# Queries, keys and values computed channel-major by the seven-product scheme, in two token halves

## The chip, the cores and the metric

One core of one Trainium2 chip. The kernel is one program with five engines that are ordered by semaphores: PE (matmul), DVE (vector), ACT (scalar, activation functions), POOL (GpSimd) and SP, which here only issues DMAs. The metric is the device time in microseconds of a run of the whole kernel, and lower is better. Time before: median 2371.23 us of three runs (2369.54 to 2375.56).

## The reference

One decoder block on 2048 tokens of 1024 channels, everything in float32. The input is normalised and modulated, projected once to 10240 columns, and split:

```
h = rms_norm(x, norm_w) * (1 + scale) + shift          # shift, scale, gate = silu(c) @ w_ada + b_ada
a, b, g_conv, q, k, v, g_attn, m_conv, m_attn = split(h @ w_in)
u = silu(layer_norm(depthwise_conv31(a * sigmoid(b)))) * silu(g_conv)
y_conv = u @ w_conv_out
q, k = rope(rms_norm(q, q_norm_w)), rope(rms_norm(k, k_norm_w))     # 12 heads of 128 channels
o = softmax-weighted sum over 3 groups of dilated_window_attention(q, k, v)
y_attn = (o * silu(g_attn)) @ w_attn_out
out = x + gate * ((sigmoid(m_conv) * y_conv + sigmoid(m_attn) * y_attn) @ w_out)
```

The three attention groups of four heads have dilations 1, 4 and 16: tokens are grouped by residue, and in each residue class a block of 128 queries attends to its own and the previous block of 128 keys. With dilation 16 a class has 128 tokens, one block. Groups 1 and 2 (dilations 4 and 16) leave an unnormalised result with its minimum and sum; group 0 comes last and joins the three.

## The kernel before

Every float32 product is made of three matmuls: weights and activations are split into a high part (rounded to fp32r by ACT) and a low part (the rest, a subtraction on DVE or POOL), and high x high, high x low and low x high are added up in PSUM.

**Start (0 to about 50 us).** x is loaded by tokens, squared and scaled on ACT, turned by PE (`pt_x` L288, `pt_first` L297); `shift` and `scale` come from products with 32 columns (L314). h stays in SBUF, channel-major, as quarters (two halves of the channels, four pieces of 512 tokens).

**Queries, keys, values (to about 1077 us).** Per head u (12, in the order of groups 1, 2, 0) and block j of 128 tokens, `project_step` makes q, k and v of the block token-major: `z_tokens` L549 does 24 matmuls of 128x384 (8 channel pieces x 3), h as the stationary side. ACT takes the sums of squares from PSUM (L572), POOL the inverse root (`rsqrt_cols` L114, L115), DVE scales from PSUM (L586) and rotates (L593 to L596). Heads of groups 1 and 2 store the block in DRAM (`qkv_d`) and load it again by residue class. Inside each set of 24 matmuls stand hooks, in which one block of attention is done in five stages, each for another block (`attend_step`): `turn_qk` L620 (two transposes), `scores` L635 with the minimum on DVE L645 and exp on ACT L647, `turn_p` L652 with its copy on DVE L654, `values` L684, `turn_o` L675. For group 0 DVE also joins the groups (L661 to L668, L686). In other hooks DVE makes the sums of h's quarters (S1 to S4, L853), which go to DRAM.

**Gates (to about 1930 us).** The columns of a, b and the gates are made channel-major in quads: 256 columns x 1024 tokens by seven products instead of eight (`quad` L1081). A quad has seven slots; in each PE does 12 matmuls of 128x512 (L1091), with weights as the stationary side. Column pieces are loaded and, in the first token half, combined into differences T1 to T4 (POOL, L1046), split (ACT L1054, DVE or POOL L1055) and the differences stored for the second half. `prepare` does this seven slots ahead, with eight buffers for split weights. A quad has its sum in three PSUM banks: `pa` (tag "z"), `pb` (tag "s") and `pc` (tag "o"), two buffers of each tag; ACT copies from `pa` to scratch (L1097), DVE adds `pb` (L1104) and `pc` (L1118), POOL adds L1115. The depthwise convolution runs on DVE, 1.5 to 3.1 steps per slot, with its sums in PSUM (tag "t"; L1140, L1153, L1169). The last blocks of attention take every second of the first 13 slots.

**Tail (to 2368 us).** Layer norm, the two output projections (L1399), merge, and output quads (L1681).

PE's instructions run in the written order (`manual_schedule`). Those of the other engines are placed by a scheduler; each engine takes its queue in order, and a waiting instruction holds up what is behind it.

## Time and profile before

| | before |
|---|---|
| median of 3 runs | 2371.23 us (2369.54 to 2375.56) |
| the profiled execution | span 2368.3 us, from its first to its last instruction; the median of the runs is 2.9 us above it |
| busy PE / DVE / ACT / POOL | 2325.8 / 1737.0 / 1020.9 / 836.1 us |
| granted TensorE clock | 1.00 in nearly every stretch |
| DMA | 378.57 MB, 160 GB/s on average |

Busy is the time in which an engine has an instruction in work. PE overlaps neighbouring matmuls, so the duration of one (349 ns for 128x384) is longer than the distance to the next one's start; what a matmul costs is that distance. Lines of groups give: line, engine, operation, output<-inputs, shape, count, then busy us and mean ns, and after the bar the idle time of the engine just before them with who ended it. Lines of a timeline give start and duration in us.

### The profile page before, as it was taken

The page shows a single profiled execution, that of the slowest core. Times are in us where ns is not written, and L with a number is a line of the kernel's source. Part 1 is how long each engine was busy: PE and PEld are TensorE (multiplying, and loading weights), DVE is VectorE, ACT ScalarE, POOL GpSimd, SP SyncE. Part 2 cuts the span into 40 slices and gives each one's busy share as a digit, 9 for nine tenths or more (in the row PEclk, how much of TensorE's full clock was granted, in tenths as well). Part 3 has the DMA queues.
Part 4 walks back from the last instruction along what each step waited for, and adds up shares of the span by engine and source line. Part 5 has one row for each costly group of instructions (what it writes and reads, how often), then busy time and mean ns, then how long its engine had stood idle before and what let it go on. Part 6 is the DMA issues. An engine that isn't in the chain of part 4 may idle for free.

```text
span 2368.3 us, 38785 instructions
## 1 busy us (share of the span) xinstructions
PE 2325.8 (98%) x12421; PEld 2083.0 (88%) x12421; DVE 1737.0 (73%) x4104; ACT 1020.9 (43%) x2825; POOL 836.1 (35%) x976
## 2 busy tenths in 40 slices
PE   6999999999999999999999999999999999999999
PEld 4899999999999999997888888788888888878887
DVE  7855655555556777776699999989968768787654
ACT  5733343343344555456444444544444444332221
POOL 4321111111111111123677778656556730000221
PEclk9999999999999999999999999999999999999999
DMA  7733544454552222144535445745444569876552
GB/s 279 241 116 117 160 125 144 149 169 149 158 162 67 60 80 67 47 123 154 170 135 176 160 152 195 241 130 151 139 150 134 165 213 330 292 236 204 185 167 102
DMA packets 354121, 378.57 MB, mean 160 GB/s; under 512 B 27688, under 2 KB 249176, under 8 KB 353918
## 3 DMA queue, kind: packets, MB, share of 16 engines
q1 hardware_dynamic: 312622, 314.05, 42.6%
q10 hardware_dynamic: 41296, 62.05, 7.5%
q8 instruction: 99, 1.62, 0.3%
q14 instruction: 104, 0.85, 0.1%
HBM read 235.34 MB, written 140.64 MB: 159 GB/s over the span
## 4 chain that ended last, share of the span: by engine, by line
PE 88%; DMA 4%; DVE 4%; ACT 2%; issue 1%; POOL 1%; SPq 0%; ACTq 0%; DVEq 0%; POOLq 0%
PE pz L549 31%; PE paab L1091 7%; PE yc L1399 6%; PE oa L1681 4%; PE pcab L1091 4%; PE pag_mc_d L1091 4%; PE pag_g_d L1091 3%; PE pag_ma_d L1091 3%; PE po L684 3%; PE ps L635 3%; PE ya L1399 2%; PE pcg_g_d L1091 2%; PE oc L1681 2%; PE pbab L1091 2%; PE paag L1091 2%; PE pcg_mc_d L1091 2%
## 5 line engine op out<-in xcount | busy, mean ns | idle before, releaser
L549 PE MATMUL pz<-wh_u,hT_lo 128*128 128x384 f32 x1504 | 525.2, 349 | 2.5 <-DVE hT_lo L371 2.4
L549 PE MATMUL pz<-wh_u,hT_hi 128*128 128x384 f32 x1504 | 505.6, 336 | 1.3 <-ACT hT_hi L369 1.3
L549 PE MATMUL pz<-wl_u,hT_hi 128*128 128x384 f32 x1504 | 505.8, 336 | 0.0
L114 POOL TENSOR_SCALAR st<-st 128x2 f32<-128x2 f32 x192 | 44.9, 234 | 797.0 <-ACT sq L572 796.7
L586 DVE SCALAR_TENSOR_TENSOR qk<-pz,st,wqk 128x128 f32<-128x128 f32 x384 | 116.9, 346 | 265.0 <-POOL st L115 260.8
L549 PEld LDWEIGHTS pz<-wh_u,hT_lo 128*128 128x128 f32 x1504 | 283.2, 188 | 4.0 <-DVE hT_lo L371 3.7
L549 PEld LDWEIGHTS pz<-wh_u,hT_hi 128*128 128x128 f32 x1504 | 283.8, 189 | 2.2 <-ACT hT_hi L369 1.9
L549 PEld LDWEIGHTS pz<-wl_u,hT_hi 128*128 128x128 f32 x1504 | 282.8, 188 | 0.5 <-issue 0.5
L627 ACT ACTIVATE qkT<-ptq 128x256 f32<-128x256 f32 x192 | 73.8, 384 | 358.1 <-PE ptq L620 302.5
L1169 DVE SCALAR_TENSOR_TENSOR ce<-us,pair_taps,ce 128x512 f32<-128x512 f32 x240 | 180.9, 754 | 6.5
L1140 DVE SCALAR_TENSOR_TENSOR ce<-ut,chan,ce 128x512 f32<-128x512 f32 x240 | 179.8, 749 | 0.0
L1055 POOL TENSOR_TENSOR slT<-wT,shT 128x512 fp32r<-128x512 f32 x107 | 143.8, 1345 | 79.8 <-ACT shT L1054 79.5
L1153 DVE SCALAR_TENSOR_TENSOR cq<-ut,chan,cq 128x512 f32<-128x512 f32 x208 | 156.0, 750 | 1.0
L1054 ACT ACTIVATE shB<-wB 128x512 fp32r<-128x512 f32 x130 | 82.1, 631 | 161.7 <-PE paab L1091 51.7
L115 POOL TENSOR_TENSOR st<-st,mhalf 128x2 f32<-128x2 f32 x192 | 140.1, 729 | 15.9
L572 ACT ACTIVATE sq<-pz 128x128 bf16<-128x128 f32 x384 | 106.1, 276 | 78.7 <-PE pz L549 68.9
L1054 ACT ACTIVATE shT<-wT 128x512 fp32r<-128x512 f32 x110 | 69.4, 631 | 160.9 <-POOL wT L1046 32.0
L1055 POOL TENSOR_TENSOR slB<-wB,shB 128x512 fp32r<-128x512 f32 x85 | 111.9, 1317 | 76.1 <-ACT shB L1054 73.8
L684 PE MATMUL po<-lv,pT 128*128 128x128 f32 x596 | 96.8, 274 | 0.0
L684 PEld LDWEIGHTS po<-lv,pT 128*128 128x128 f32 x596 | 90.9, 190 | 0.6 <-issue 0.5
L593 DVE TENSOR_TENSOR t<-qk,tab 128x256 f32<-128x256 f32 x192 | 82.5, 430 | 5.7
L1055 POOL TENSOR_TENSOR slT<-wB,shT 128x512 fp32r<-128x512 f32 x57 | 75.1, 1324 | 28.4 <-ACT shT L1054 28.3
(783 smaller groups left out, 6163.2 us busy)
## 6 DMA issues: line engine op xcount, KB each, us to landing
wB<-in_w_in_dram SPq DMA_DIRECT2D x154, 256.0 KB, 3.2
qkv_d<-qkv SPq DMA_DIRECT2D x128, 192.0 KB, 2.3
wT<-tT_d SPq DMA_DIRECT2D x88, 256.0 KB, 2.7
tT_d<-wB ACTq DMA_DIRECT2D x66, 256.0 KB, 2.7
lqk<-qkv_d SPq DMA_DIRECT2D x128, 128.0 KB, 2.3
raw_u<-in_w_in_dram SPq DMA_DIRECT2D x84, 192.0 KB, 3.6
acc_d<-osb SPq DMA_DIRECT2D x128, 65.0 KB, 2.0
part<-acc_d ACTq DMA_DIRECT2D x64, 130.0 KB, 2.4
```

Of the source, the lines that this page charges most:

```text
L115: nc.gpsimd.tensor_tensor(dst, scratch[:, :n], mhalf[:, :n], op=ALU.pow)
L549: nc.tensor.matmul(pz[:, :width], part(a, k, P * j, P), w[:, :width], start=(m == 0), stop=(m == 23))
L586: nc.vector.scalar_tensor_tensor(qk[:, 2 * i : 2 * i + 2].rearrange("p a b -> p (a b)"), pz[:, P * i : P * i + P], st[:, 2 + i : 3 + i], w ...
L684: nc.tensor.matmul(po[:, :P], box["pT"][:, P * i : P * i + P], vt, start=(i == 0), stop=(i == nk - 1))
L1054: nc.scalar.activation(h, q[name], AF.Copy)
L1055: eng.tensor_tensor(l, q[name], h.bitcast(F32), op=ALU.subtract)
L1091: nc.tensor.matmul(ps, w, x, start=(m == 0 and ps.name not in first), stop=(m == 11 and not more), skip_group_check=True)
L1140: stt(box["e"], e[:, 1 + j : 513 + j], chan[:, cb, 2 * j : 2 * j + 1], box["e"], op0=ALU.mult, op1=ALU.add)
L1153: stt(box["o"], o[:, 2 + j : 514 + j], w, psum_o, op0=ALU.mult, op1=ALU.add)
L1169: stt(dst, box["both"][:, 1 + j : 513 + j], pair_taps[:, cb, j : j + 1], box["e"], op0=ALU.mult, op1=ALU.subtract if j == 0 else ALU.add)
L1399: nc.tensor.matmul(pz, w, xx, start=(m == 0), stop=(m == len(terms) - 1))
L1681: nc.tensor.matmul(ps, y, w, start=(m == 0 and ps.name not in begun), stop=(m == 11 and not more), skip_group_check=True)
```

## The change

**Projection.** `z_tokens`, `project_step` and the token-major q, k and v are gone. The columns of q, k and v are made by the same `quad` as the gates (now L260, matmul L270). A head pair has three quads for a half of 1024 tokens: 256 columns of q, of k and of v. The host permutes the columns of q and k, so that one 128-column piece holds the first 64 channels of both heads and the other the last 64. Each token half does 18 such quads and then its 22 gate quads, 40 jobs of seven slots; before, the halves were split only for the gates. The host also lays w_in out in 128-column tiles and gives x a second time, channel-major.

**After a quad.** `turn_v` (L447) turns v by 16 transposes in the four slots after the quad. `rotate` (L467) takes q and k: squares on ACT, sums over a head's 128 channels by f32 matmuls with the 32-column matrix `sel` (L490), through DRAM to a tile of 16 columns, inverse root on POOL, through DRAM back to rows that are broadcast; the rotation's 12 operations on DVE (L503 to L511), and the scaling (L534). The steps are dealt out to slots +1 to +8 after the quad's end. q, k and v go to DRAM channel-major (`qk_d`, `v_d`) and come back by block.

**Attention.** `attend` (L545) has no `turn_qk`. Its stages (load, fetch, scores, turn_p, values, turn_o) go forward by one in each slot, between two products; a new block is entered in three of four slots in the projection and in every slot of the gates, from 10 or 11 slots after the pair's last quad. Two residue classes of group 2 share a block (64 tokens of each in a half; `mask2`), and in half 1 their keys of half 0 are a second key block. The copy of the output went from DVE to ACT.

**Buffers.** The PSUM tags have 2, 1, 2 and 3 banks; `pb` and `pc` of a quad share the one bank "s". Split weights have five buffers, not eight, and are prepared four slots ahead. The low parts of q, k and v's weights are POOL's. The convolution runs at 3.1 steps per slot throughout. The first two quads run interleaved; between their products stand the start's second parts (`start_a`, `start_b`), and h of half 1 is made in slots 5 to 37.

The core of the diff (the new functions are printed in parts):

```diff
...
+WS = 5
...
+    BANKS = {"z": 2, "s": 1, "t": 2, "o": 3}
...
+        return psum.tile([P, 512], F32, tag=tag, name=name, bufs=BANKS[tag])
...
+    sel = consts.tile([P, 32], F32, name="sel")
+    nc.gpsimd.memset(sel, 0.0)
+    nc.gpsimd.memset(sel[:64, 0:1], 1.0 / P)
+    nc.gpsimd.memset(sel[64:, 1:2], 1.0 / P)
...
+    def quad(name, got, sink, place=None, cut=lambda x: x, side="s"):
...
+        pb = bank(side, f"pb{name}")
+        product(1, pb)
+        nc.vector.tensor_tensor(s1, s1, cut(pb), op=ALU.add)
+        sink(0, 0, s1)
...
+        pc = bank(side, f"pc{name}")
+        product(3, pc, True)
...
+    def qkv_quad(half, which, pair, got, side):
+        u0 = 2 * pair
+        g = GROUPS[u0 // NH]
+        reg = [scratch_pair() for _ in range(2)]
...
+        def sink(t, col, z, free=None):
+            if (t, col) == (1, 0):
+                (turn_v if which == 2 else rotate)(half, which, u0, g, reg, n)
+
+        return quad(n, got, sink, place, cut, side)
...
+        for i in range(4):
+            def f(col=i // 2, c=i % 2):
...
+                for b in range(4):
+                    nc.tensor.transpose(pt[:, P * b : P * b + P], reg[col][:, 512 * c + P * b : 512 * c + P * b + P], ident)
...
+        def squares(c):
+            box["sq", c] = []
+            for i, x in enumerate(reg):
+                sq = rp["p"].tile([P, 512], F32, tag="sq", name=f"sq{n}_{c}{i}", bufs=2)
+                nc.scalar.activation(sq, x[:, 512 * c : 512 * c + 512], AF.Square)
+                box["sq", c].append(sq)
...
+        def sums(c):
+            pr = bank("t", f"pss{n}_{c}")
+            for i, sq in enumerate(box.pop(("sq", c))):
+                for q in range(4):
+                    nc.tensor.matmul(pr[32 * q : 32 * q + 32, :P], sel, sq[:, P * q : P * q + P], start=(i == 0), stop=(i == 1))
...
+                    stt(t[0], xa, wA, cs, op0=ALU.mult, op1=ALU.mult)
+                    stt(t[1], xb, wB, sn, op0=ALU.mult, op1=ALU.mult)
+                    stt(xa, xa, wA, sn, op0=ALU.mult, op1=ALU.mult)
...
+                    stt(xb, xb, wB, cs, op0=ALU.mult, op1=ALU.mult)
...
+                    tt(fb, fb, fa, op=ALU.add)
+                    tt(fa, t[0], t[1], op=ALU.subtract)
...
+        def roots():
...
+            rsqrt_cols(st[:, 32:48], st[:, :16], 16, st[:, 16:32])
...
+        def spread():
...
+                nc.sync.dma_start(rs[64 * h : 64 * h + 64], rs_d[h][None, :].to_broadcast([64, HS]))
...
+        def scaled(i):
+            x = reg[i]
+            tt(x, x, box["rs"], op=ALU.mult)
+            for h in range(2):
+                nc.sync.dma_start(qk_d[u0 + h][half, 64 * i : 64 * i + 64, which], x[64 * h : 64 * h + 64])
+
+        squares(0)
+        for d, f in ((1, lambda: sums(0)), (1, lambda: squares(1)), (2, lambda: sums(1)), (2, part(0, 0)), (3, roots), (3, part(0, 1)),
+                     (4, part(1, 0)), (5, part(1, 1)), (5, spread), (7, lambda: scaled(0)), (8, lambda: scaled(1))):
+            at_slot(s0 + d, f)
...
-    def z_tokens(pz, width, wh, wl, j, hooks):
...
-    def project_step(u, j, cs, wts, hooks, hold=False):
...
-    def attend_step(u, j, qkv, state, hold=False):
...
+    def attend(half, u, b, state):
...
+            inner, cross = False, b if half else None
+        nk = 2 if inner or cross is not None else 1
...
-        on_vector = range(7) if i < 3 else () if half else (0, 5)
+        on_vector = () if half or kind is qkv_quad else (0, 5)
...
+    LEAD = WS - 1
...
-            running[i] = kind(*job, columns[i][0])
+            running[i] = kind(*job, columns[i][0], "o" if i in seconds else "s")
         next(running[i], None)
-        prepare(at + 7)
...
-        if at < TAIL and at % 2 == 0:
-            if own:
-                main.enter(own.pop(0))
-            for f in main.turn():
-                f()
...
+        prepare(s + LEAD)
+        for f in agenda.pop(s, ()):
+            f()
+        if waiting and (s % 4 != 3 or i % half_jobs >= QJ):
+            main.enter(attend(*waiting.pop(0)))
+        for f in main.turn():
+            f()
...
-        due += 2.9 if i < half_jobs - 2 else 1.5 if i < half_jobs + 2 else 3.1
+        due += 3.1
+        if not conv_todo:
+            due = 0.0
...
+    w = given["w_in"][:, order].reshape(2, 4, P, -1, P).transpose(3, 0, 2, 1, 4).reshape(-1, 2, P, 4 * P)
...
+    add("xt", given["x"].reshape(S, KC, P).transpose(1, 2, 0))
...
```

PE's order, before: within the 24 matmuls of one block (here `pz_3`), a hook with stages of four blocks of attention (`po` values, `ptp` turn_p, `ps` scores, `ptq` the turned q and k).

```order
L549 MATMUL pz_3_5154<-wl_u_4_4408,hT_hi_201 128x384
L684 MATMUL po_12_5169<-lv_12_4805,pT_12_5107 128x128
L652 MATMUL ptp_13_5173<-ident,sm_13_5113 128x128 x2
L635 MATMUL ps_14_5178<-qkT_13_5046,qkT_14_5119 128x128
L635 MATMUL ps_14_5178<-qkT_14_5119 128x128
L620 MATMUL ptq_15_5185<-ident,lqk_15_5008 128x128 x2
L549 MATMUL pz_3_5154<-wh_u_4_4407,hT_lo_202 128x384
```

After: between products 0 and 1 of the quad `q_3` (pair 3's q, half 0).

```order
L270 MATMUL paq_3_2838<-A_hi_343,slB_0_4352_2701 128x512
L453 MATMUL ptv_2_00_2862<-ident,spare_hi 128x128 x4
L598 MATMUL ptp_0_0_2870<-ident,sm_0_0_2831 128x128
L583 MATMUL ps_0_4_2874<-qk_0_0_2762,qk_0_4_2797 128x128
L583 MATMUL ps_0_4_2874<-qk_0_4_2797 128x128
L270 MATMUL pbq_3_2881<-A_hi_533,shB_0_4352_2734 128x512
```

The transposes of q and k are gone, those of the quad before (`ptv_2`) stand there, and the stages are between products, one step per 12 matmuls of 512 columns.

DVE's order in the projection, before: one block's rotation (`qk`, `t`, `qkv`) with the attention of another block between.

```order
L586 SCALAR_TENSOR_TENSOR qk_3_5210<-pz_3_5154,st_3_5203,wqk 128x128 x2
L593 TENSOR_TENSOR t_3_5213<-qk_3_5210,tab_112 128x256
L594 TENSOR_TENSOR qkv_3_5206<-qk_3_5210,tab_112 128x256
L690 COPY osb_13_5112<-po_13_5238 128x128
L654 COPY pT_14_5246<-ptp_14_5243 128x256
L595 TENSOR_TENSOR qkv_3_5206<-qkv_3_5206,t_3_5213 128x2x64
L596 TENSOR_TENSOR qkv_3_5206<-qkv_3_5206,t_3_5213 128x2x64
```

After: the rotation of pair 2's q (in `spare_hi`, with temporary tiles `tmq`) around the add of `pbk_2`, the second product of the next quad (L284).

```order
L503 SCALAR_TENSOR_TENSOR tmq_2_00_2307<-spare_hi,hw,cos_665 128x512
L504 SCALAR_TENSOR_TENSOR tmq_2_01_2308<-spare_hi,hw,sin_666 128x512
L505 SCALAR_TENSOR_TENSOR spare_hi<-spare_hi,hw,sin_666 128x512
L507 SCALAR_TENSOR_TENSOR spare_hi<-spare_hi,hw,cos_665 128x512
L600 COPY pT_0_3_2265<-ptp_0_3_2263 128x128
L510 TENSOR_TENSOR spare_hi<-spare_hi 128x512
L511 TENSOR_TENSOR spare_hi<-tmq_2_00_2307,tmq_2_01_2308 128x512
L503 SCALAR_TENSOR_TENSOR tmq_2_10_2389<-spare_hi,hw,cos_665 128x512
L504 SCALAR_TENSOR_TENSOR tmq_2_11_2390<-spare_hi,hw,sin_666 128x512
L284 TENSOR_TENSOR spare_lo<-spare_lo,pbk_2_2271 128x32x16
L505 SCALAR_TENSOR_TENSOR spare_hi<-spare_hi,hw,sin_666 128x512
```

Eight operations of the rotation, of 512 columns each and with inputs in SBUF, stand ahead of the add.

ACT's order at the first gate quad with Silu (`g_d`), before: table loads between Silu (L1217) and the exponential (L647).

```order
L1217 ACT_TABLE_LOAD
L1217 ACTIVATE spare_hi<-spare_hi 128x512
L1054 ACTIVATE shT_0_2304_15222<-wB_0_2304_15050 128x512
L1097 ACTIVATE spare_hi<-pag_g_d_0_15069 128x512
L1218 DMA g_d<-spare_hi 128x512
L1059 DMA tT_2304_d<-wB_0_2304_15052 128x512
L627 ACTIVATE qkT_2_15207<-ptq_2_15202 128x256
L647 ACT_TABLE_LOAD
L647 ACTIVATE sm_1_15199,stm_1_15198<-sm_1_15199,stm_1_15198 128x256
```

After, at the same gate quad (Silu is L402, the exponential L593).

```order
L402 ACT_TABLE_LOAD
L402 ACTIVATE spare_hi<-spare_hi 128x512
L593 ACT_TABLE_LOAD
L593 ACTIVATE sm_0_4_5808,stm_0_4_5807<-sm_0_4_5808,stm_0_4_5807 128x256
L608 ACTIVATE stm_0_4_5807<-stm_0_4_5807 128x3
L403 DMA g_d<-spare_hi 128x512
L232 ACTIVATE shT_0_2304_5889<-wB_0_2304_5597 128x512
L613 ACTIVATE part_0_4_5755<-part_0_4_5755,stm_0_4_5807 128x128
L402 ACT_TABLE_LOAD
```

The two functions alternate for as long as group 0's attention lasts: ACT's order has 48 table loads, 8 before.

More of the change, by code (lines that the diff above doesn't have):

```diff
@@ L1122, in quad @@
         product(6, pa)
+        if place:
+            kept(pa, 1, 0)
         sink(1, 0, pa, s1)
@@ L1208, in sink, with gate_quad @@
                 conv_todo.extend(conv_parts(half, cb, ut))
-        return quad(f"ab{half}_{cb}", got, sink)
-    def gate_quad(half, g, cb, got):
+        return quad(f"ab{half}_{cb}", got, sink, side=side)
+    def gate_quad(half, g, cb, got, side):
         _, dst, func = g
@@ L1345, in tile_hybrid_block @@
+        prepare(s + LEAD)
[4 more added lines that the diff above has]
+        for f in main.turn():
+            f()
+        for half in range(2):
+            if last_turn[half] and s > last_turn[half] + 10 and not waiting and not main.parts:
+                last_turn[half] = 0
+                attention_shut()
+        while held and held[0][0] <= s:
             held.pop(0)[1]()
```

1511 lines of the change are left out of this document (641 added, 870 removed).

## The prediction

> **What bounds the kernel now.** I read the page first, its engine totals, its slices and the chain of work that ended last; then the busy time in stretches; then single instructions on the timeline.
>
> ```profile
> PE 2325.8 (98%) x12421; PEld 2083.0 (88%) x12421; DVE 1737.0 (73%) x4104; ACT 1020.9 (43%) x2825; POOL 836.1 (35%) x976
> ...
> PE   6999999999999999999999999999999999999999
> ...
> DVE  7855655555556777776699999989968768787654
> ...
> PE 88%; DMA 4%; DVE 4%; ACT 2%; issue 1%; POOL 1%; SPq 0%; ACTq 0%; DVEq 0%; POOLq 0%
> ```
>
> PE is busy in every slice after the first, and 88% of the chain is PE itself. The stretches show whose reserve is how large (a row gives the stretch, then busy us and instructions of PE, weight loads, DVE, ACT and POOL):
>
> ```profile
> 0.00:25.00 25.00, 11.89 (x88) 6.19 (x89) 18.25 (x38) 12.38 (x22) 7.10 (x18) 1.00 0.93 325
> 200.00:400.00 200.00, 200.00 (x1291) 199.04 (x1290) 117.69 (x410) 76.76 (x314) 34.52 (x74) 1.00 0.46 137
> 1077.00:1125.00 48.00, 42.59 (x214) 35.21 (x213) 31.55 (x83) 33.56 (x72) 15.54 (x16) 1.00 0.50 163
> 1200.00:1400.00 200.00, 200.00 (x884) 165.62 (x883) 188.35 (x278) 84.66 (x149) 146.65 (x120) 1.00 0.46 152
> ```
>
> In the token-major phase (200 to 400) PE has no gap, and DVE, ACT and POOL have much to spare. In the gates phase (1200 to 1400) PE is still full, but DVE has 12 us of 200 left. PE loses time only at the start and at the change between the two (1077 to 1125: 5.4 us). So PE's own instructions set the time, and an instruction taken from PE is worth its issue spacing, as long as nothing else becomes late. The change must be judged by both: PE work removed, and waits made.
>
> **PE work, removed and added.** Matmuls overlap, so a record's duration isn't its price; the distance between starts is. Token-major matmuls, and the attention step that follows them:
>
> ```profile
> 301.13 0.34 PE L549 MATMUL pz<-wl_u,hT_hi 128*128 128x384 f32 x1
> ...
> 304.77 0.34 PE L549 MATMUL pz<-wl_u,hT_hi 128*128 128x384 f32 x1
> 304.95 0.61 PE L684 MATMUL po<-lv,pT 128*128 128x128 f32 x4
> 305.39 0.27 PE L652 MATMUL ptp<-ident,sm 128*128 128x128 f32 x1
> 305.50 0.39 PE L635 MATMUL ps<-qkT,qkT 128*128 128x128 f32 x2
> ```
>
> From 301.13 to 304.77 are 21 steps: 0.1733 us each. Four 128-column records take 0.44 us: 0.11 each. The seven-product quads, in the gates phase before and also the end of its first half:
>
> ```profile
> 1503.97 0.39 PE L1091 MATMUL pag_ma_d<-hT_hi,shT 128*128 128x512 f32 x1
> ...
> 1508.50 0.39 PE L1091 MATMUL pag_ma_d<-hT_hi,slT 128*128 128x512 f32 x1
> 1513.01 0.79 PE L1091 MATMUL paab<-A_hi,shB 128*128 128x512 f32 x1 [4.12 <-ACT spare_hi L1217]
> 1513.60 0.63 PE L1091 MATMUL paab<-A_lo,shB 128*128 128x512 f32 x1
> ```
>
> Twenty steps in 4.53 us: 0.2265 each. Counts of matmuls come from the code; these rows and the two below price the sum:
>
> ```profile
> L549 PE MATMUL pz<-wh_u,hT_lo 128*128 128x384 f32 x1504 | 525.2, 349 | 2.5 <-DVE hT_lo L371 2.4
> ...
> L620 PE MATMUL ptq<-ident,lqk 128*128 128x128 f32 x382 | 73.2, 273 | 5.7 <-DVE pT L654 3.5 <-DVE lqk L596 2.2
> ```
> ```profile
> 35.89 1.50 PE L314 MATMUL ada<-first_lo,first_hi 128*32 128x256 f32 x24
> 37.32 0.98 PE L387 MATMUL pz<-wh_u,hT_hi 128*128 128x384 f32 x4
> ```
>
> - Projection: 12 heads x 16 blocks x 24 = 4608 matmuls (three groups of 1504 at L549 and 96 in the start) x 0.1733 = 798.6 us. After: 36 quads x 84 = 3024 x 0.2265 = 684.9. **-113.7.**
> - The 384 transposes of q and k (382 in the row) x 0.11 = **-42.2**: channel-major q and k need none. The 128 transposes of x go too: **-14.1**.
> - v is now turned by 192 transposes: **+21.1**.
> - Two residue classes of group 2 share a block, so 32 blocks get a second key block that holds nothing unmasked but its half: scores and values 0.22 each, transpose 0.11: 32 x 0.55 = **+17.6**.
> - Head norms by matmul with `sel`: 384 f32 matmuls with 32 columns, 768 records. In the row above 24 records of 256 columns took 1.43 us (37.32 - 35.89), 0.06 each; with 128 columns between half of that and all of it: 23 to 46, I take **+26**, nearer to half.
> - Squares of x by 64 f32 matmuls, 128 records at no more than 0.11: **+14**.
>
> Sum **-91 us**. Everything else on PE (44 gate quads, attention's other matmuls, the output products) keeps its count.
>
> **What is late next.** Four places, each costed from both sides.
>
> *Start and first quads: +12 (0 to 27).* The first 25 us are DMA-bound (share 0.93) before, and load about as much after. But there is no attention yet under the first six quads, and POOL makes every lo part, the four weight differences and one add per quad: 12 operations.
>
> ```profile
> L1055 POOL TENSOR_TENSOR slT<-wB,shT 128x512 fp32r<-128x512 f32 x57 | 75.1, 1324 | 28.4 <-ACT shT L1054 28.3
> ...
> L115 POOL TENSOR_TENSOR st<-st,mhalf 128x2 f32<-128x2 f32 x192 | 140.1, 729 | 15.9
> ```
>
> 12 x 1.324 = 15.9 us per quad; in slots 3 to 42 (5.7 quads) 91 us, ten lo parts of the four sums 13 more, and three rotations some 23 (a power of 16 columns, not seen before: above 0.73, under 8 x 0.73, taken as 2; the rest is waiting, next place): 127. PE needs 5.7 x (84 x 0.2265 + 0.9) = 113. Excess 14, with a few slots' lead.
>
> *Rotation against POOL: +25 (0 to 102).* Single instructions on POOL, then on DVE, in one stretch:
>
> ```profile
> 1500.40 1.75 POOL L1115 TENSOR_TENSOR spare_lo<-spare_lo 128x512 f32<-128x512 f32 x1
> 1502.11 1.75 POOL L1055 TENSOR_TENSOR slB<-wB,shB 128x512 fp32r<-128x512 f32 x1
> 1503.83 1.28 POOL L1115 TENSOR_TENSOR spare_lo<-spare_lo 128x512 f32<-128x512 f32 x1
> ```
> ```profile
> 1502.62 0.74 DVE L1140 SCALAR_TENSOR_TENSOR ce<-ut,chan,ce 128x512 f32<-128x512 f32 x1
> 1503.28 0.75 DVE L1153 SCALAR_TENSOR_TENSOR cq<-ut,chan,cq 128x512 f32<-128x512 f32 x1
> 1503.93 1.73 DVE L896 TENSOR_TENSOR S_lo<-landingS,S_hi 128x512 fp32r<-128x512 f32 x1
> ```
> ```profile
> L1055 DVE TENSOR_TENSOR slT<-wB,shT 128x512 fp32r<-128x512 f32 x9 | 6.1, 687 | 3.0 <-ACT shT L1054 3.0
> ```
>
> `S_lo` reads two SBUF tiles; started just after a POOL operation, it ends 0.58 us after that one ends and takes 1.73 instead of 0.69, and the POOL operations it got between took 1.75 instead of 1.28. Convolution steps, whose accumulator is in PSUM, keep 0.75 beside the same POOL work. The page "SBUF — State Buffer" of the Trainium skill (section "SBUF: two separate sides") speaks against this change: a DVE operation with two SBUF inputs and a GpSimd operation that reads SBUF exclude each other for the whole instruction, whoever starts first. By that rule the trace agrees on DVE's side, while POOL lost 0.47, not DVE's whole 0.69.
>
> The old rotation begins from PSUM (L586), in small pieces, beside a POOL that is 17% busy (34.52 of 200). The new one is 12 operations of two SBUF inputs per quad of q or k, 24 quads, and in DVE's order eight of them stand before the add of the next quad's second product. That add frees the only "s" bank, which product 3 needs. DVE up to that add: about 1 us until the squares have been read, 9 x 0.69 = 6.2, and two attention steps, for which these rows give 0.83 each:
>
> ```profile
> L645 DVE CUSTOM_DVE_ANT_0 sm<-ps,mask 128x256 f32<-128x256 f32 x108 | 45.0, 418 | 0.0
> L654 DVE COPY pT<-ptp 128x256 f32<-128x256 f32 x108 | 44.8, 416 | 0.0
> ```
>
> That is 8.9 us, against three slots of 12 x 0.2265 + 0.55 = 9.8. Slack 0.9. Each POOL operation met costs 1.73 - 0.69 = 1.04. In half 0 POOL has some 3.3 operations in that stretch, in half 1 two (the differences come from DRAM). If all collide: (3.4 - 0.9) x 12 + (2.1 - 0.9) x 12 = 44; if few do, nothing. I take 25.
>
> *Attention under the gates: +20 (0 to 52).* Group 0's blocks of each half now run beside its first gate quads, and ACT alternates Silu and Exp: 48 table loads in the program, 8 before.
>
> ```profile
> 1101.59 0.63 ACT L1217 ACTIVATE spare_hi<-spare_hi 128x512 f32<-128x512 f32 x1
> 1102.24 1.28 ACT L647 ACT_TABLE_LOAD   x1
> 1103.53 0.51 ACT L647 ACTIVATE sm<-sm,stm 128x256 f32<-128x256 f32 x1
> ```
>
> A switch costs 1.31 us between the two neighbours (1102.22 to 1103.53). 40 x 1.3 = 52 if PE waits for each; nothing if ACT's reserve (115 us of 200 in the gates) hides them. Before, five loads fell into 1077 to 1125, where PE lost 5.4 in all, at most 1.1 each; I take 0.5 each. The page "ScalarE: Activation LUTs" of the Trainium skill (section "What ACT_TABLE_LOAD costs") has 2.66 us for a switch, load and drain; by that the upper end would be an estimated 106 us. The measured 1.31 shows the load and no drain. DVE meets the same stretch with 12 us in 200 to spare and 32 steps of at least 0.83 (27 us) per half, which is why I don't go lower.
>
> *Changes of phase: +5 (0 to 10).* There are three (projection to gates, gates to projection, projection to gates) instead of two; one cost 5.4. The 4.12 us gap at 1513 with the slow matmuls behind it (0.59 instead of 0.23 apart) belongs to the change of halves, which stays.
>
> At nothing: the quarter sums of half 1 and its h (made and stored from slot 5 to 37, used after slot 280), the channel-major stores and loads on SP, issued two or more slots ahead,
>
> ```profile
> qkv_d<-qkv SPq DMA_DIRECT2D x128, 192.0 KB, 2.3
> ```
>
> and the head norm's round trip: four transfers one after another at 2.3 us and the power make 11 us, and slots +3 to +7 give 13. Without that cover the scaling waits in DVE's queue with adds and attention behind it; that lies inside the 102.
>
> **The sum.** -91 + 12 + 25 + 20 + 5 = -29. The profiled execution spans 2368.3 us; the median of the runs, 2371.2, is 2.9 above it, and I set the sum on the median: **2342 us**.
>
> **Rivals.**
> - *All gain, no new wait* (13%): 2371 - 91 = 2280. For it: DVE and ACT had 41% and 62% to spare in 200 to 400. Against: slack of 0.9 us and the collisions above.
> - *Slower: POOL falls behind and stays behind* (21%). If POOL's queue never empties in half 0, all eight rotation operations ahead of the add meet one: 8 x 1.04 - 0.9 = 7.4 us of PE per quad, x 12 = 89, and 14 for half 1: 103 instead of 25: 2342 + 78 = 2420. It decides from 61 us, 2.5 us for each of 24 quads, on. For it: POOL's 127 of 113 in the first quads leaves it behind. Against: with attention a quad takes some 23 us (84 x 0.2265, 0.9 for sums and 0.55 in three of four slots), in which POOL's 16 to 23 fit, and splits are paced by five weight buffers.
> - *The gates become DVE's* (12%): the convolution keeps 3.1 steps per slot beside attention. The 27 us of a half meet 6% reserve, 6 us in a stretch of 100; 21 us show in each half, 42 instead of 20: 2364, the edge of no change, and up to 2378 with the loads on top. For it: 188 of 200. Against: the lo parts that DVE made in the first gates of before are POOL's now.
> - *It doesn't do what it says*: excluded, the order of PE has 3024 more products of 512 columns and none of 384.
>
> **How the numbers follow.** Forecast 54% (2300 to 2364), all gain 13%, no change 12%, slower 21%. A measurement of this kernel tells 0.3% (7 us) from no change, so faster means under 2364, slower over 2378: 0.67, 0.12, 0.21. The range leaves out the best case's lower half and the upper part of the slow one: **2283 to 2408**.
>
> **What would show it.** PE's 512-column spacing 0.2265 with no gaps in the projection, and PE's busy time some 90 us below 2326 with some 60 us more idle, would confirm the work sum. The `s1` adds late (over 1 us behind product 1), rotation operations at 1.0 to 1.7 us and PE idle at product 3, released by that add, would confirm the second place; the same in every q and k quad of half 0 at 5 us or more is the slow rival. Gaps behind table loads confirm the third. If PE waits for weights (lo parts on POOL, or DMAs) all through half 0, or if the start loses 30 us more, my places are the wrong ones.

## The result: slower by 12.7%

The changed kernel takes 2673.7 us (median of four runs, 2667.3 to 2679.8) against 2372.9 us before (four runs): a ratio of 1.127, 95% interval 1.125 to 1.129. The forecast was 2342 with a range that ended at 2408.

The profile after, page and chain:

```profile
PE 2390.2 (89%) x11580; PEld 1940.7 (73%) x11580; DVE 1842.7 (69%) x3034; ACT 1184.5 (44%) x2313; POOL 1300.8 (49%) x1014
...
PE   6766788988888999999888899888999998999999
...
DVE  2779655555588999995755444459899985777744
...
PEclk7787889999999999999989999999999999999999
...
PE 34%; DVE 5%; DMA 4%; issue 2%; ACT 1%; SPq 1%; POOL 0%; ACTq 0%; DVEq 0%; POOLq 0%
```

PE has fewer instructions and more busy time, which looks like a contradiction and isn't: busy time counts slow matmuls too, and in the rows below the granted clock (the third figure from the end) is 0.79 to 0.94 in the stretches in which PE has gaps and 1.00 in the one in which it has almost none. No other engine is full (DVE 69%, POOL 49%, ACT 44%). So no engine took PE's place as the bound; PE waits, in many places, for engines that are themselves waiting. The stretches, with the same columns as before:

```profile
0.00:136.00 136.00, 94.04 (x449) 73.49 (x450) 65.85 (x80) 56.88 (x90) 65.86 (x65) 0.79 0.50 175
136.00:286.00 150.00, 98.08 (x449) 74.83 (x449) 119.66 (x93) 66.27 (x100) 100.36 (x56) 0.81 0.64 187
286.00:658.00 372.00, 324.90 (x1756) 261.59 (x1755) 204.70 (x341) 167.44 (x403) 239.85 (x167) 0.93 0.56 162
658.00:834.00 176.00, 141.26 (x723) 116.12 (x722) 123.29 (x377) 106.57 (x231) 66.95 (x82) 0.93 0.50 152
834.00:1174.00 340.00, 333.95 (x1479) 275.79 (x1477) 320.28 (x461) 158.39 (x279) 257.09 (x206) 1.00 0.53 178
1174.00:1709.00 535.00, 476.49 (x2613) 389.19 (x2614) 291.32 (x422) 246.90 (x509) 259.99 (x173) 0.94 0.55 158
```

The row that a reader should stop at is 834 to 1174, the gates of half 0 alone: DVE has 320 of 340 us, the heaviest load of any stretch, and PE loses nearly nothing. In the projection (286 to 658) DVE has 55% and PE has gaps throughout. A load isn't a wait; what is queued ahead of what PE needs can be one, and the experiments ask for that.

For the rest I count PE's loss thus: from each matmul's start to the next one's, less 0.2267 us for 512 columns (0.1733 for 384, 0.11 for 128 or fewer). What is over by more than 0.35 us is a gap, what is over by less (but by more than 0.01) a slow matmul. A gap belongs to the stretch in which it begins.

| stretch | what runs | gaps + slow, us | most of the gaps stand before |
|---|---|---|---|
| 0 to 136 | start | 72 | the third product, the squares of x |
| 136 to 286 | first quads | 70 | turn_v, first copies, adds |
| 286 to 658 | projection, half 0 | 86 | turn_p 26, values 19 |
| 658 to 834 | attention beside gates | 53 | scores 18, turn_p 10, turn_o 9 |
| 834 to 1174 | gates | 7 | |
| 1174 to 1709 | change, projection half 1 | 105 | turn_p 26, values 24 |
| 1709 to 1869 | attention beside gates | 35 | scores 11, turn_o 8 |
| 1869 to 2672 | gates, tail | 35 | |

In all 463 us, 308 in gaps and 155 in slow matmuls, of which 119 lie within 6 us after a gap; before it was 84 (42 and 41), of which 41 in the first 286 us and 21 from there to 1077. From first to last matmul that leaves 2200 us of work after and 2276 before: 76 less. So 463 - 84 - 76 = 303; the two spans differ by 304.

Where PE waits, by the view of waits:

```profile
PE ptp L598 <- ACT sm L593: 57.8, 39, 5.2
PE po L620 <- DVE pT L600: 34.9, 16, 4.9
PE paq L270 <- ACT spare_hi L276: 18.1, 3, 14.1
PE ptv L453 <- ACT vev L455: 17.9, 3, 10.1
PE pck L270 <- DVE spare_lo L284: 17.5, 4, 6.4
```

Only the last is the wait on which the prediction's second place was built (product 3 behind the add). The first two are attention's stages. One such stall, on the timeline of PE, then DVE, ACT and POOL:

```profile
334.58 0.39 PE L583 MATMUL ps<-qk 128*128 128x128 f32 x2
...
337.35 0.39 PE L270 MATMUL pak<-S_hi,slT 128*128 128x512 f32 x1
342.30 0.69 PE L598 MATMUL ptp<-ident,sm 128*128 128x128 f32 x2 [4.56 <-ACT sm L593]
342.78 0.64 PE L583 MATMUL ps<-qk 128*128 128x128 f32 x2
343.07 0.77 PE L270 MATMUL pck<-S_hi,shT 128*128 128x512 f32 x1
343.64 0.63 PE L270 MATMUL pck<-S_lo,shT 128*128 128x512 f32 x1
```
```profile
335.50 0.69 DVE L511 TENSOR_TENSOR spare_hi<-tmq,tmq 128x512 f32<-128x512 f32 x1
336.22 1.10 DVE L503 SCALAR_TENSOR_TENSOR tmq<-spare_hi,hw,cos 128x512 f32<-128x512 f32 x1
337.25 1.07 DVE L504 SCALAR_TENSOR_TENSOR tmq<-spare_hi,hw,sin 128x512 f32<-128x512 f32 x1
338.25 1.05 DVE L284 TENSOR_TENSOR spare_lo<-spare_lo,pbk 128x512 f32<-128x512 f32 x1
339.22 1.06 DVE L505 SCALAR_TENSOR_TENSOR spare_hi<-spare_hi,hw,sin 128x512 f32<-128x512 f32 x1
340.21 1.06 DVE L507 SCALAR_TENSOR_TENSOR spare_hi<-spare_hi,hw,cos 128x512 f32<-128x512 f32 x1
341.19 0.41 DVE L592 CUSTOM_DVE_ANT_0 sm<-ps,mask 128x256 f32<-128x256 f32 x1
```
```profile
341.64 0.51 ACT L593 ACTIVATE sm<-sm,osb 128x256 f32<-128x256 f32 x1 [6.81 <-DVE osb L592]
342.06 0.19 ACT L593 ACTIVATION_READ_ACCUMULATOR sm<-sm,osb 128x1 f32 x1
342.15 0.61 ACT L232 ACTIVATE shB<-wB 128x512 fp32r<-128x512 f32 x1
```
```profile
333.08 1.84 POOL L233 TENSOR_TENSOR slT<-wB,shT 128x512 fp32r<-128x512 f32 x1 [1.21 <-ACT shT L232]
342.84 1.27 POOL L233 TENSOR_TENSOR slB<-wB,shB 128x512 fp32r<-128x512 f32 x1 [7.93 <-ACT shB L232]
```

The scores are ready at about 335. Their minimum (`sm`, L592) stands on DVE behind six operations, five of them rotation, and comes at 341.2. The exponential waits in ACT's queue; behind it waits the high part of a weight (`shB`), and behind that POOL, idle for 7.93 us. PE stands still 4.56 us and then runs at 0.43 us per matmul until 348, for which the profile has a granted clock of 0.50:

```profile
341.50:348.00 6.50, 5.71 (x16) 4.64 (x17) 2.12 (x7) 2.57 (x6) 5.00 (x4) 0.50 0.00 0
```

POOL was idle while the rotation ran here, and still four of these operations took 1.06 to 1.10 us.

### The profile page after: what moved, and what is told of

The parts are those of the page before. It is cut to its first block, busy times and chain, and to the rows that moved or that the text cites. A ratio compares the mean times of both kernels' runs of the same rounds, so it can differ in the third digit from the quotient of the medians.

```text
span 2672.6 us, 36779 instructions
## 1 busy us (share of the span) xinstructions
PE 2390.2 (89%) x11580; PEld 1940.7 (73%) x11580; DVE 1842.7 (69%) x3034; ACT 1184.5 (44%) x2313; POOL 1300.8 (49%) x1014
## 5 line engine op out<-in xcount | busy, mean ns | idle before, releaser
L233 POOL TENSOR_TENSOR slB<-wB,shB 128x512 fp32r<-128x512 f32 x196 | 271.8, 1387 | 342.0 <-ACT shB L232 289.5
L233 POOL TENSOR_TENSOR slT<-wT,shT 128x512 fp32r<-128x512 f32 x200 | 278.5, 1393 | 213.5 <-ACT shT L232 186.8
L233 POOL TENSOR_TENSOR slT<-wB,shT 128x512 fp32r<-128x512 f32 x120 | 171.7, 1441 | 109.8 <-ACT shT L232 74.2
L232 ACT ACTIVATE shT<-wT 128x512 fp32r<-128x512 f32 x200 | 125.9, 629 | 214.3 <-issue 20.9
L600 DVE COPY pT<-ptp 128x256 f32<-128x256 f32 (+1 forms) x192 | 73.2, 382 | 175.7 <-PE ptp L598 175.0
L227 POOL TENSOR_TENSOR wB<-wB,wB 128x512 f32<-128x512 f32 x80 | 112.8, 1410 | 54.8 <-DVE slB L233 49.8
L593 ACT ACTIVATE sm<-sm,osb 128x256 f32<-128x256 f32 (+1 forms) x128 | 59.8, 467 | 168.1 <-DVE osb L592 143.4
L598 PE MATMUL ptp<-ident,sm 128*128 128x128 f32 x332 | 74.5, 295 | 58.8 <-ACT sm L593 57.8
L620 PE MATMUL po<-v,pT 128*128 128x128 f32 x560 | 99.0, 285 | 23.1 <-DVE pT L600 20.7
L232 ACT ACTIVATE shT<-wB 128x512 fp32r<-128x512 f32 x120 | 75.3, 628 | 99.2 <-PE pbab L270 11.1
L592 DVE CUSTOM_DVE_ANT_0 sm<-ps,mask 128x256 f32<-128x256 f32 (+1 forms) x192 | 73.1, 381 | 63.0 <-PE ps L583 38.5
L620 PEld LDWEIGHTS po<-v,pT 128*128 128x128 f32 x560 | 86.3, 197 | 36.4 <-DVE pT L600 24.8
L583 PE MATMUL ps<-qk 128*128 128x128 f32 x384 | 79.7, 292 | 0.7 <-DVE osb L622 0.7
```

The lines of the kernel that those rows point to most:

```text
L227: nc.gpsimd.tensor_tensor(dst, x0, x1, op=ALU.subtract)
L232: nc.scalar.activation(h, q[name], AF.Copy)
L233: eng.tensor_tensor(l, q[name], h.bitcast(F32), op=ALU.subtract)
L583: nc.tensor.matmul(ps[:, P * i : P * i + P], box["q"], kt, start=True, stop=True)
L598: nc.tensor.transpose(pt[:, P * i : P * i + P], box["sm"][:, P * i : P * i + P], ident)
L620: nc.tensor.matmul(po[:, :P], box["pT"][:, P * i : P * i + P], vt, start=(i == 0), stop=(i == nk - 1))
```

## The experiments

Each kernel is the changed one with one edit, run once beside the kernel before; runs of the changed kernel itself lie 12 us apart, so less than that is nothing, and the prices below are good to about as much. "Lost" is counted as above.

### What DVE has in its queue

Without the rotation (e1):

```diff
+                return
                 xa, xb = rows(A, c), rows(B, c)
```

> Leaves out the 12 rotation operations per quad of q and k on DVE (q and k go on unrotated); norm, scaling, stores and all else stay. Theory A (bursts of rotation in DVE's in-order queue hold up adds and the attention stages behind them): PE's loss in the two projections (92 us early, 73 in half 0, 73 in half 1, slow matmuls included) falls by more than half, time 2673 - 110 to 170 = 2505 to 2565. Theory B (SP's in-order queue is what everybody waits for): within 30 us of 2673.

Measured 2615.2, 58 us less. The loss in the projections went from 86 to 63 and from 105 to 84 only. Both theories missed: the rotation has a price, but half of what theory A asked.

Without the low parts of the projection's weights on POOL (e2):

```diff
-            eng.tensor_tensor(l, q[name], h.bitcast(F32), op=ALU.subtract)
+            if c0 < Q0 or c0 >= GA0:
+                eng.tensor_tensor(l, q[name], h.bitcast(F32), op=ALU.subtract)
+            else:
+                l = h
```

> Leaves out the low parts of the weights of q, k and v on POOL (the high part is used in their place; PE's matmuls stay), so seven POOL operations per quad of the projection are gone and DVE's rotation meets fewer of them. Theory A with exclusion against POOL as its main price: rotation operations go from 1.0-1.4 us back to 0.75-1.06 and the time falls by 60 to 110 us (2565 to 2615). Theory A with the queue's order as the main price, whatever POOL does: 15 to 45 us (2630 to 2660). Theory B: under 15 us.

Measured 2615.1, also 58 less, just outside the range for exclusion. The rotation's operations, after and in this run (L507 is L510 there, L505 is L508):

```profile
L507 DVE SCALAR_TENSOR_TENSOR spare_lo<-spare_lo,hw,cos 128x512 f32<-128x512 f32 x24 | 33.2, 1383 | 0.4
...
L505 DVE SCALAR_TENSOR_TENSOR spare_hi<-spare_hi,hw,sin 128x512 f32<-128x512 f32 x24 | 26.1, 1086 | 1.2 <-DVE tmk L503 0.5 <-ACT sqq L483 0.3
```
```profile
L510 DVE SCALAR_TENSOR_TENSOR spare_lo<-spare_lo,hw,cos 128x512 f32<-128x512 f32 x24 | 26.2, 1093 | 1.0 <-ACT sqk L486 0.7
...
L508 DVE SCALAR_TENSOR_TENSOR spare_hi<-spare_hi,hw,sin 128x512 f32<-128x512 f32 x24 | 24.0, 1001 | 2.5 <-ACT sqq L486 2.0
```

In these two rows POOL's share is the difference, 0.1 to 0.3 us, and the larger part of the excess over 0.69 stays. Over all 288 operations of the rotation it is about half: they take 336 us in the kernel and 269 here, and 288 x 0.69 would be 199. What stays is mostly the strided tables (last section).

The page "SBUF — State Buffer" of the Trainium skill (section "SBUF: two separate sides") states that a DVE operation with two SBUF inputs and a GpSimd operation that reads SBUF shut each other out for the whole instruction. The rows of the first quads agree in kind: the same DVE line took 2.17 us with one of POOL's low parts in work at its start, and 1.22 without:

```profile
149.27 2.17 DVE L930 SCALAR_TENSOR_TENSOR cos<-na,cos 128x1024 f32<-128x1024 f32 x1
151.47 1.22 DVE L930 SCALAR_TENSOR_TENSOR cos<-sin,cos 128x1024 f32<-128x1024 f32 x1
```

So POOL has a price here, 58 us with everything that hangs on it: the first quads lose 46 us instead of 70, the two projections 76 instead of 86 and 78 instead of 105. That is a fifth of the slowdown. The run doesn't separate longer DVE operations from weights that are ready sooner.

One slot more between scores and turn_p (e4):

```diff
-        return (load, fetch, scores, turn_p, values, *((turn_o,) if g == 0 else ()))
+        return (load, fetch, scores, lambda: None, turn_p, values, *((turn_o,) if g == 0 else ()))
```

> One empty slot more between scores and turn_p of each attention block (with a third buffer for the exponentials, one more for v and for the output). Theory A: DVE's delay is then met by 3 us of slack, PE's waits at turn_p (19 us in half 0, 25 in half 1, and slow matmuls behind them) go and the time falls by 40 to 80 us (2593 to 2633). Theory B: what turn_p waits for comes late by itself, so less than 15 us.

Measured 2673.4: nothing. The waits moved on: in e4 PE waits for the next stage instead (57.8 for turn_p and 34.9 for values in the kernel itself):

```profile
PE po L620 <- DVE pT L600: 70.9, 26, 11.6
```

The waits for turn_p are gone and nothing is won. I read this as DVE's queue being late and not one stage, since each stage comes through that queue; e6 bears on it.

Without rotation and scaling (e6), without scaling alone (e9), and with the scaling done but nobody waiting (e13):

```diff
-            tt(x, x, box["rs"], op=ALU.mult)
```

In e6 and e9 the line is left out, in e6 with e1's edit beside it; e13 multiplies by a table of cosines that is there already, so its values aren't the norm's:

```diff
-            tt(x, x, box["rs"], op=ALU.mult)
+            tt(x, x, rp["cos"], op=ALU.mult)
```

> Leaves out the rotation and also the multiplication by the root (the round trip through DRAM still runs, nobody on DVE waits for it). Theory A2 (whatever stands or waits in DVE's in-order queue ahead of attention is the price, and after the rotation it is the scaling that waits for the broadcast rows): 30 to 70 us less than without rotation alone, 2545 to 2585. Rival (one slot per stage is too short for attention, whatever else DVE does): within 15 us of 2615.

> Leaves out only the multiplication of q and k by the root; the rotation stays on DVE, and the round trip runs with nobody waiting for it. If the scaling's wait (18 to 28 us from the sums to the rows, where 13 were provided) is a price of its own: as much as from no rotation to no rotation and no scaling, 110 us less, about 2563. If rotation and scaling fill one queue and either one's absence is enough for part of it: 40 to 75 us less, 2598 to 2633.

> The scaling multiplies by the cosine table instead of the rows of roots: the same two DVE operations of 1024 columns per quad, in the same places, but nobody waits for the round trip through DRAM. If the wait is what the scaling costs (18 to 28 us of round trip where 13 were provided): near the run without scaling, 2590 to 2620. If DVE's time for it is (54 us in all, stretched by POOL): 2645 to 2675.

Measured: e6 2505.0 (169 less), e9 2597.5 (76 less), e13 2626.8 (47 less). e6 won more than theory A2 asked (110 on top of e1, not 30 to 70); e9 lies just past the upper end of its second range. So the scaling costs about 76, of which about 47 are the wait for the rows and 29 DVE's time; e13 lies between its two ranges for that reason. The two parts together give more (169) than each alone (58 + 76 = 134): with either one in the queue, part of the other's delay shows. With both out, the projection of half 0 is nearly tight, PE 301 of 306 us:

```profile
256.00:562.00 306.00, 301.16 (x1751) 246.86 (x1752) 61.26 (x216) 166.39 (x400) 216.50 (x163) 0.99 0.67 196
```

Its loss is 21 us instead of 86, that of half 1 31 instead of 105. POOL (71%), ACT and SP have the same work here as in the kernel, so none of them sets this phase by its work alone. DVE's collisions with POOL go too in e6, but they aren't the whole of it: e2, which takes most of them away, wins 10 and 27 us in the two projections, e6 65 and 74.

### The round trip of the norm

The wait is that for the rows of roots. DVE stands idle 64 us in all before the scaling, waiting for these rows (us in all, times):

```profile
  DMA rsk<-rsk_d: 36.1, 11
  DMA rsq<-rsq_d: 27.7, 8
```

One trip, from the sums (ACT) through DRAM to the scaling, in the timeline:

```profile
637.27 0.26 ACT L493 ACTIVATE ssrk<-pssk 128x128 f32<-128x128 f32 x1
...
640.74 2.02 SPq L517 DMA_DIRECT2D ssk_d<-ssrk  x3
645.86 0.53 SPq L519 DMA_DIRECT2D stk<-ssk_d  x1
...
650.67 2.94 POOL L136 TENSOR_TENSOR stk<-stk,mhalf 128x16 f32<-128x16 f32 x1
653.64 0.33 SPq L527 DMA_DIRECT2D rsk_d<-stk  x1
...
656.80 1.11 SPq L530 DMA_DIRECT2D rsk<-rsk_d  x2
...
661.38 2.36 DVE L534 TENSOR_TENSOR spare_hi<-spare_hi,rsk 128x1024 f32<-128x1024 f32 x2 [2.90 <-DMA rsk<-rsk_d]
```

24.1 us. Over the 24 quads it is 18 to 29 us, but for the first three (27 to 42). Of it, in this trip: 8.6 until the load of the sums is issued (the stores of the sums and then their load stand behind other issues on SP), 4.8 until the power starts (the load lands, and POOL has differences of weights ahead of the power), 2.9 for the power, 3.2 until the broadcast is issued, 4.6 until DVE has it.

The scaling on POOL (e10):

```diff
-            tt(x, x, box["rs"], op=ALU.mult)
+            nc.gpsimd.tensor_tensor(x, x, box["rs"], op=ALU.mult)
```

The trip asked for one slot sooner (e14, with e3's edit below):

```diff
-        for d, f in ((1, lambda: sums(0)), (1, lambda: squares(1)), (2, lambda: sums(1)), (2, part(0, 0)), (3, roots), (3, part(0, 1)),
-                     (4, part(1, 0)), (5, part(1, 1)), (5, spread), (7, lambda: scaled(0)), (8, lambda: scaled(1))):
+        for d, f in ((1, lambda: sums(0)), (1, lambda: squares(1)), (2, lambda: sums(1)), (2, part(0, 0)), (2, roots), (3, part(0, 1)),
+                     (4, spread), (4, part(1, 0)), (5, part(1, 1)), (7, lambda: scaled(0)), (8, lambda: scaled(1))):
```

> The multiplication by the root is POOL's instead of DVE's; everything is computed. Theory: the wait then stands in POOL's queue, whose low parts are four slots ahead, and attention and adds no longer stand behind it on DVE: 40 to 90 us less, 2583 to 2633. Rival: POOL (64% busy in half 0) falls behind with the low parts and PE waits for weights instead: within 25 us of 2673, or more.

> Everything is computed. The round trip is asked for one slot sooner (sums to DRAM at +2, roots back at +4), and the stores of v and of attention are ACT's as in the run with that change alone (2651). If the wait for the round trip is the price: another 20 to 50 us less, 2600 to 2630. If SP's queue and POOL set its length whatever the slot: within 12 us of 2651.

Measured: e10 2676.7, no change; e14 2657.7, no gain on e3's 2650.7. In e10 the attention's waits fell (turn_p from 26 to 10 in half 0), but PE now waits for copies into scratch, which has room for two quads: a quad's columns are held until they are scaled and stored. In the same stretch of e10:

```profile
PE paq L270 <- ACT spare_hi L276: 12.1, 2, 9.9
PE pav L270 <- ACT spare_hi L276: 10.2, 2, 9.1
```

ACT's copies into scratch wait 45 us for those stores (`qk_d`) in e10, 27 in the kernel. There is a second price: the scaling takes 129 us in all on POOL and 77 on DVE, and the rotation beside it goes from 336 to 407 us. How much of e10's result is the ring of buffers and how much this isn't separated. In e14 the trip isn't shorter: 20.9 us on average from the fourth quad on, 20.7 in e3. That fits a trip that stands in the queues of SP and POOL whatever the slot. A trip with empty queues wasn't tried.

### SP, tables, convolution, start

The stores of v and of attention's output issued by ACT instead of SP (e3; the three stores of attention in the same way):

```diff
-                nc.sync.dma_start(v_d[u0 + col][half, c], ve)
+                nc.scalar.dma_start(v_d[u0 + col][half, c], ve)
```

Tanh in place of Silu, so that no table changes (e5):

```diff
-            nc.scalar.activation(th, z, func, scale=1.0 if func == AF.Silu else 0.5)
+            nc.scalar.activation(th, z, AF.Tanh, scale=0.5)
```

Most of the convolution's steps left out (e8):

```diff
-        return [*[even(j) for j in range(HT + 1)], add, *[odd(j) for j in range(HT)], join,
-                *[mixed(j) for j in range(HT + 1)], done]
+        return [even(0), add, odd(0), odd(HT - 1), join, mixed(0), mixed(HT), done]
```

> v's stores, the stores of unnormalised attention results and those of the finished ones are issued by ACT, which makes these tiles, instead of SP. Theory B: v's stores no longer stand behind SP's other waits, loads get through earlier: 40 us or more less (under 2635). Theory A: within 15 us (2658 to 2688), with the waits of turn_v in the first 200 us gone at most.

> The gate g_conv uses Tanh in place of Silu, so ACT has no reason to change tables beside the attention of group 0. Table theory: the two stretches in which attention runs beside gate quads (53 us lost in half 0, 35 in half 1) lose half as much: 20 to 45 us less, 2628 to 2653. Theory that DVE (convolution and group 0's joining in one queue) or the three banks of tag o hold them: under 10 us.

> Leaves out 41 of the 46 convolution steps of each column block. Theory that DVE's queue is what holds attention beside the gates: the loss there (53 and 35 us) halves, 25 to 45 us less, 2628 to 2648. Table theory: under 10 us there. The pure gates phases lose little (7 and 12 us) and can give at most that.

Measured: e3 2650.7 (23 less), e5 2646.2 (27 less), e8 2655.1 (19 less). Theory B asked for 40 of e3, so SP's order is a cause, not the cause. e5 lies in the range of its theory, e8 (25 to 45) below it. Beside the gates the loss of 53 and 35 us falls to 35 and 22 without table changes and to 42 and 29 without most of the convolution: both matter, tables perhaps more. All 40 extra loads at 1.28 us come to 51; about half showed.

The start, without the reduction of the sine's angles (e7; the rest of the same chain goes too):

```diff
-        yield lambda: v.tensor_scalar(n, a, 1.0 / (2 * math.pi), MAGIC, op0=ALU.mult, op1=ALU.add)
...
```

Without the sums of quarters at the start, quarters themselves in their place (e11):

```diff
-        for k in range(4):
-            x11, x12, x21, x22 = hf[k, 0], hf[4 + k, 0], hf[k, 1], hf[4 + k, 1]
-            tt(x22, x21, x22, ALU.add)
-            tt(x21, x11, x21, ALU.subtract)
-            tt(x11, x22, x11, ALU.subtract)
-            part_of("S2", k, x11, nc.vector)
...
+        for name, same in (("S2", "A12"), ("S1", "A11"), ("S3", "A22"), ("S4", "A12")):
+            quarters[name] = quarters[same]
```

Without the making of half 1's h beside the first quads, and without its loads at the change of halves (e12):

```diff
-    for j in range(8):
-        at_slot(6 + j, lambda j=j: later_x(j))
-        at_slot(8 + j, lambda j=j: later_square(j))
-    at_slot(17, later_root)
...
```

> Leaves out the 13 DVE operations that reduce the angles (1024 columns each, 2.2 us beside POOL, 1.2 alone) in slots 5 to 18; sine and cosine are taken of the unreduced angles. Theory: this chain is what holds ACT (sine waits in ACT's queue, the copies of v behind it) and DVE's adds between 136 and 286 us, where 70 us are lost: 25 to 55 us less, 2618 to 2648. Rival (h of half 1 made in slots 5 to 37, and POOL's queue): under 15 us.

> Leaves out the sums of half 0's quarters at the start (A11, A12 and A22 stand in for S1 to S4), so PE's third product needs no sum of all four quarters. Theory: the scheme's third product, which needs every part of x, is what the first 136 us lose (72 us against 35 in the kernel before): 25 to 50 us less, 2623 to 2648, with the gap of 8.8 us at 84 gone. Rival (the loads, the modulation and POOL's weights set that pace): under 10 us.

> Leaves out h of half 1 (half 0's quarters are used twice), so nothing of it runs in slots 5 to 37 and nothing is loaded at the change of halves. Theory: this work on DVE, ACT and SP beside the first quads is what the stretch from 136 to 286 us loses (70 us): 20 to 40 us less, and 10 to 20 at the change of halves: 2613 to 2643 together. Rival (first quads wait for POOL's weights and rotation whatever else): under 10 us in that stretch.

Measured: e7 2669.6 (nothing), e11 2663.9 (10 less, within the spread), e12 2642.6 (31 less). The theories of e7 and e11 missed; e12 lies just inside its range. In e7 the 18 us of turn_v went, and the same time came back as waits for the adds and copies. In e11 the start lost 51 instead of 72, and the first quads 76 instead of 70. In e12 the first quads lost 46 instead of 70 and the change of halves some 6 less. e1, e2 and e6 help here too: the first quads lose 54 without rotation, 46 without POOL's low parts, 40 without rotation and scaling. The first 286 us have several causes in a row, and taking away one shows the next; which one would be last isn't settled.

### All of it

Everything above that paid, taken out together (e15: e1, e9, e3, e12, e5, e8).

> Leaves out all that was taken out one by one: rotation, scaling, h of half 1, Silu (Tanh stands for it) and most of the convolution, and issues the stores on ACT. The single gains add up to 169 + 31 + 27 + 19 + 23 = 269: 2404 if they are independent. If the places share one wait (each removal shows the next): 2430 to 2480. If what is left is only start and tail (PE's work of some 2200 and 95 us): 2300 to 2340.

Measured 2407.8, against 2404 by adding up. As groups the causes add up, and without them 266 of the 301 us are gone. That isn't a price that a complete kernel could save: rotation, scaling, half 1's h and most of the convolution are work that the kernel before has too, and hides. What is left, 197 us of loss, is the start (71), the first quads (23), the tail (24; 23 in the kernel) and some 80 us spread over the rest.

## Why the prediction was wrong

Its sum against the runs, in its own terms. Measured are the losses of the table less the 84 us of the kernel before, 41 of them in the first 286 us, 21 from there to 1077:

| term | forecast | measured |
|---|---|---|
| PE's work | -91 | -76 |
| start, first quads | +12 | +101 |
| rotation against POOL; round trip at nothing | +25 | +170 |
| attention under the gates | +20 | +88 |
| changes of phase; tail at nothing | +5 | +20 |
| sum | -29 | +303 |

**PE's work: right.** -91 forecast, -76 by this count. 0.2267 per 512-column matmul held, and in the gates PE lost next to nothing. What failed is the waits.

**"At nothing: ... the head norm's round trip" failed.** It had four transfers at 2.3 us and a power of 2, 11 us in 13 provided. It measured 18 to 29 (24.1 in the trip shown): four landing times leave out the queue in which each transfer is issued and the engine between, and SP and POOL had others ahead. The prediction named what it would cost without that cover ("the scaling waits in DVE's queue with adds and attention behind it") and then didn't price it: about 47 us for the wait alone, 76 with DVE's work for the scaling, which is in no term of its sum.

**"Rotation against POOL: +25" was mis-sized, and its victim was the wrong one.** Rotation and scaling cost 169, POOL's low parts 58 of the whole (e2). First the operation: 0.69 us was taken from a contiguous one. Groups 1 and 2 read the tables in steps of 4 and 16 columns, and such operations took 1.06 to 1.18 with POOL idle; with POOL's share the mean over all 288 was 1.17 (336 us). The collisions themselves are there. (The rows at 1503 give 0.55 us for its 0.58; that changes nothing.) Then the wait: the step followed DVE only to the add that frees the bank, and gave it 9.8 us. The scores' minimum, the copy of the transposed exponentials and, through ACT, the weights' high parts are in the same queues and have one slot of some 3.3 us: turn_p and values have 96 of the 117 us of gaps in the two projections, the add that the prediction followed some 10. The order shown in the section on the change has `pT` between rotation operations; it was there to be read.

**A gap was priced at its own length.** The row at 1513 showed slow matmuls after a 4 us gap; it was called part of the change of halves and left at that. Here 308 us of gaps came with 155 us of slow matmuls, most of them right behind a gap.

**Start and first quads: +12 against 101.** POOL's load was counted (127 of 113 us), and it has a part: without its low parts the first quads lose 46 of 70. Left out were DVE's and ACT's queues, which hold the sine, the sums of half 1, the copies of v and the adds in one line each, while PE's first quads have nothing else to do, because attention isn't there yet. Which of them weighs most stays open.

**Attention beside gates: +20 against 88.** Tables cost 27 (0.7 us a load, 0.5 forecast), convolution 19; the rest, scores behind group 0's operations on DVE and copies on ACT that free the three banks of tag "o", was not taken apart.

**The tail, at nothing.** It lost 23 us against 9 before, 15 of it ahead of `ya`. No run looks into it.

**The slow rival** had the right place and sign. Its collisions are there (e2), but its condition isn't: POOL's queue did empty (64% busy in half 0; in the stall shown it waited 7.93 us for ACT), and no wait of PE for POOL's weights stands in the profile. Its price of 78 was too low, because every reserve was taken as an average. DVE had 41% to spare in 200 to 400 before, and has 45% in 286 to 658 now; in the stall shown a queue of six operations ahead of one minimum made the difference.

## What to carry to other kernels

When work is moved from many small operations to a few long ones on an engine that also serves a pipeline with one slot per stage, price the longest run of operations ahead of each stage in that engine's order, not the engine's load. A round trip through DRAM takes its transfers plus the queues of every engine that issues or computes in between; here that came to about twice the sum of the landing times. And price a gap on PE with the slow matmuls behind it.

## What the hardware showed that was not expected

- A table read in steps cost these DVE operations half as much again. The same line, POOL idle in both rows, took 1.07 us in a quad of group 2, which reads the cosines in steps of 16 columns, and 0.74 in one of group 0, which reads them in one piece:

```profile
473.50 1.07 DVE L507 SCALAR_TENSOR_TENSOR spare_hi<-spare_hi,hw,cos 128x512 f32<-128x512 f32 x1
...
523.73 0.74 DVE L507 SCALAR_TENSOR_TENSOR spare_hi<-spare_hi,hw,cos 128x512 f32<-128x512 f32 x1
```

- The power on POOL takes longer with more columns: 16 columns took 2.94 us (`stk` above), 2 columns 0.73 before; the forecast had 2.
- A scaling of 1024 columns took 1.22 us alone and 2.3 beside POOL, once 3.04.
